# Expert outputs stored by row in DRAM and fetched by token, a mixture-of-experts gather in four parts, and dense up products with both activation parts in one matmul

## The chip, the core and the metric

The kernel runs on one core of a Trainium2 chip. The metric is the device time of one execution in microseconds (us). Five engines work side by side, each through its own instruction queue in order: TensorE (PE; its weight loads are listed apart as PEld), VectorE (DVE), ScalarE (ACT), GpSimd (POOL) and SyncE (SP, which here issues only transfers). An engine whose next instruction waits holds up everything behind it in its queue.

## What is computed

Two transformer-like blocks over 256 tokens of width 1024. The parts that the change touches:

```
def swiglu(h, w_gate, w_up, w_down):                      # dense, D_FF = 2816
    return (jax.nn.silu(h @ w_gate) * (h @ w_up)) @ w_down

def moe_swiglu(h, router_w, router_b, w_gate, w_up, w_down):   # 8 experts, top 2 per token
    ...
    out = jnp.zeros_like(h)
    for e in range(N_EXPERTS):
        out = out + gates[..., e:e + 1] * swiglu(h, w_gate[e], w_up[e], w_down[e])
    return out
...
# second block, MLP with D_FF_2 = 4096
m = jnp.einsum('bsf,fd->bsd', jnp.square(jax.nn.relu(jnp.einsum('bsd,df->bsf', h, w_up[l]))), w_down[l])
```

In order: a convolution block (A), the dense swiglu (B), attention (C), the mixture of experts (D), a mixer of attention and a gated delta net (F), and the MLP (G).

## The kernel before

**Two-part products.** Every float32 operand of a large product is split in a rounded high part and a low remainder (`split`: ACT copies the high part, DVE subtracts). A product is three matmuls, high by high, high by low, low by high (`mm3`), summed in PSUM. Weights come in tiles of 1 MiB (`raw`, a ring of 4 buffers, transfers issued by SP); each is split in two halves of 1024 columns (`whi` by ACT, `wlo` by DVE, rings of 6), so PE's matmuls wait for ACT and DVE, and SP's next transfer waits for DVE to be done with a `raw` buffer.

**Dense up products** (blocks B and G). The normalised activations lie transposed in SBUF, high parts in two tiles (`hhi`), low parts in two others (`hlo`). One up product of 256 features (`lin_feat`) runs over 2 feature halves and 8 slices of the model width, 3 matmuls of 256 columns each: 48 matmuls into one PSUM bank of 512 columns. Block B makes 22 of them (gate and up in 11 chunks), block G 15 in this way (the first of its 16 chunks goes through `lin_first`, which stays). After them DVE multiplies the bank by the norm's factor, ACT takes the silu, and so on, and the down product of the chunk before follows (24 matmuls of 512 columns).

**Mixture of experts** (`moe_block`). An expert has room for 128 tokens. For a pair of experts a one-hot matrix `G` (DVE) picks the tokens: `gather` multiplies it with the stored activations (32 matmuls of 256 columns, in 4 banks, each emptied by ACT and DVE into `xg`). Each expert then has 11 chunks: 24 matmuls of 512 columns into `pgu` (gate and up side by side), `gated` (ACT, then DVE) into `msg`, two transposes (`mpt`), a split into `mhi` and `mlo`, and the down product, 12 matmuls into the expert's two `acc` banks. The transposes and the down product of a chunk are emitted inside the next chunk. After an expert's last down product `scatter` splits `acc` (ACT `yhi`, DVE `ylo`), multiplies it with the transposed one-hot `GT` (8 matmuls of 512 columns, `scat`), and DVE adds gate times result to the residual `x` in 4 instructions. A branch in expert 0 (`overflow`) holds a second pass for experts with more than 128 tokens. In the last expert the constants of the mixer are loaded through POOL (`mixer_consts`).

**What sets the order.** The Tile framework orders each engine's instructions when the program is built; `tc.issue_after` pins single ones. In a chunk the two transposes stand either after 12 of the 24 `pgu` matmuls or right after the first; the built order of before has them after 12 in 57 of the 88 chunks and after the first in 31.

Of the kernel before, what the change touches and what calls it, by code (L numbers as in the profile page):

```python
# [14 lines left out]
P = 128  # L15
# [17 lines left out]
def _const_tables():  # L33
# [30 lines left out]
    put("low", np.tile((e[None, :] < e[:, None]).reshape(1, 64), (P, 1)))  # L64
    put("qsc", np.where(p < 8, 0.125, 1.0)[:, None])
# [37 lines left out]
def kernel(ctx: ExitStack, tc: tile.TileContext, ins: dict, out: bass.AP):  # L103
# [244 lines left out]
    class Feed:  # L348
# [3 lines left out]
        def __init__(self, *gains):  # L352
            self.gains, self.views, self.wait, self.rs, self.bc = gains, None, [], [None, None], {}
            self.early, self.pre = {}, {}
            self.stats, self.stats_late = [], False

        def piece(self, tb, half, x):
            if self.views is None:
                self.views = [hT_view(*hT_tiles("h")) for _ in self.gains]
# [26 lines left out]
        def convert(self, g, tb, half, ps_):  # L386
            hi, lo = self.views[g]
# [398 lines left out]


    def ffn_block(x, feed, nxt):
# [218 lines left out]
    def moe_block(x, feed, nxt):  # L1007
# [28 lines left out]
        def one_hots(e):  # L1036

            G = [wk("G", T, F32R) for _ in range(2)]
            for j in range(2):
                for tb in range(2):  # L1040
# [6 lines left out]
        def gather(G, n, hi, lo):  # L1047

            per = 512 // n
            for b in range(KD // per):  # L1050
# [10 lines left out]

        def scatter_mat(G, GT, r, ps_):

            for tb in range(2):
                pe.transpose(ps_[:, tb * P:(tb + 1) * P], f(G[tb]), ident)
            for tb in range(2):
                mm(ps_[:, 256:257], f(G[tb]), rs[tb], tb == 0, tb == 1)
            act.activation(GT, ps_[:, :T], AF.Copy)
            act.activation(r, ps_[:, 256:257], AF.Copy)

        def gated(sg, pgu, r):
            act.activation(sg, pgu[:, 0:256], AF.Silu, scale=r)  # L1072
            stt(sg, pgu[:, 256:512], r, sg, ALU.mult, ALU.mult)
# [85 lines left out]

        jobs = {}  # L1160

        def start(e):
            if e % 2 == 0:
                jobs["G"] = one_hots(e)
                hi, lo = [[b4("xg", F32R) for _ in range(2)] for _ in range(2)]
                jobs["pair"] = [[t[k // 4][:, (k % 4) * 256:(k % 4 + 1) * 256] for k in range(KD)] for t in (hi, lo)]
                gather(jobs["G"], 256, *jobs["pair"])
            o = slice((e % 2) * P, (e % 2 + 1) * P)
            J = dict(xg=[[t[:, o] for t in h] for h in jobs["pair"]], r=sm("rse", 1, bufs=3),
                     GT=kpool.tile([P, T], F32R, tag="gt", name=nm("GT"), bufs=2),  # L1170
# [11 lines left out]
        def down(p):  # L1182
# [9 lines left out]
            if c == NCH - 1:  # L1192
# [5 lines left out]
        pend = None  # L1198
        start(0)
        for e in range(NE):  # L1200
            for c in range(NCH):
# [10 lines left out]
                gated(sg, pgu, J["r"])  # L1212
# [484 lines left out]
    def mlp_block(x, feed, nxt):  # L1697
# [17 lines left out]
        for c in range(n):  # L1715
# [19 lines left out]
    def feed_of(st):  # L1735
# [20 lines left out]
        fd.soon = st == "G"  # L1756
# [101 lines left out]
```

## Time and profile before

| | us |
|---|---|
| median of 3 runs | 1704.89 |
| lowest, highest run | 1704.25, 1707.17 |
| the profiled execution, its own time | 1699.43 |
| span of the profiled execution | 1697.7 |
| PE busy in the span | 1625.0 (96%) |
| DVE busy | 1250.7 (74%) |
| ACT busy | 1016.9 (60%) |

The span runs from the first to the last instruction; the time of an execution has 1.7 us more around it. Busy shares are averages over stages with different limits. The mixture of experts fills the span from about 471 to 1282 us, block B about 140 to 340 us, block G about 1505 to 1690 us.

### The profile page before, as it was taken

What the parts mean: (1) busy time and instruction counts of PE and PEld (TensorE: products, weight loads), DVE (VectorE), ACT (ScalarE), POOL (GpSimd) and SP (SyncE); (2) the same over time, 40 slices, a digit from 0 to 9 for tenths busy, and PEclk for the clock granted to TensorE, in tenths of its full rate; (3) what the DMA queues carried; (4) which work ended last, traced back from release to release, by engine and by line L of the source; (5) the groups of instructions that cost most, each with busy time, mean ns of one, the idle gap of its engine ahead of it and who ended that gap; (6) DMA issues with size and microseconds to landing.
All of it is one profiled execution on the core that took longest, in us unless ns stands there. A gap on an engine that the chain in (4) does not pass through costs nothing.

```text
span 1697.7 us, 26302 instructions
## 1 busy us (share of the span) xinstructions
PE 1625.0 (96%) x10450; PEld 1375.9 (81%) x10450; DVE 1250.7 (74%) x1738; ACT 1016.9 (60%) x1464; POOL 78.9 (5%) x113
## 2 busy tenths in 40 slices
PE   7999999999889999999999999999998988989998
PEld 6769999898778788777878778787777877879997
DVE  4466555676578998989988898989887775385554
ACT  4245444565467777777777777777676454354442
POOL 2400000000000000000000000000000000011111
PEclk9989999999899999999999999999999998999999
DMA  6655555435528889999999998899995341035551
GB/s 237 186 181 192 178 194 177 175 133 199 199 103 324 323 335 355 343 351 352 335 337 352 373 356 335 338 349 341 361 354 186 125 142 46 3 139 200 196 180 45
DMA packets 59973, 408.71 MB, mean 241 GB/s; under 512 B 7353, under 2 KB 7745, under 8 KB 12609
## 3 DMA queue, kind: packets, MB, share of 16 engines
q1 hardware_dynamic: 56448, 396.86, 63.4%
q0 software_dynamic: 3104, 9.55, 2.0%
q8 instruction: 85, 1.39, 0.3%
q10 hardware_dynamic: 288, 0.52, 0.1%
q14 instruction: 48, 0.39, 0.1%
HBM read 404.67 MB, written 2.24 MB: 240 GB/s over the span
## 4 chain that ended last, share of the span: by engine, by line
PE 60%; DVE 5%; ACT 3%; issue 2%; DMA 1%; POOL 0%; DVEq 0%; POOLq 0%; ACTq 0%
PE pgu L145 27%; PE acc L145 18%; PE pu L145 6%; DVE wlo L156 2%; PE pi L145 2%; PE paq L145 1%; ACT whi L167 1%; PE pqkv L145 1%; PE mpt L1178 1%; PE scat L145 1%; DMA raw<-in_moe_w_down_dram 1%; ACT xg L1058 0%; DVE qkv L159 0%; DVE Vi L156 0%; PE po L145 0%
## 5 line engine op out<-in xcount | busy, mean ns | idle before, releaser
L156 DVE TENSOR_TENSOR wlo<-raw,whi 128x1024 fp32r<-128x1024 f32 x752 | 890.8, 1222 | 254.7 <-ACT whi L167 246.8
L167 ACT ACTIVATE whi<-raw 128x1024 fp32r<-128x1024 f32 x752 | 761.1, 1057 | 256.0 <-PE pu L145 71.8
L145 PE MATMUL pgu<-whi,xg 128*128 128x512 f32 x1408 | 467.7, 398 | 5.9 <-DVEq L1106 4.1
L145 PEld LDWEIGHTS pgu<-whi,xg 128*128 128x128 f32 x1408 | 265.6, 189 | 63.2 <-PEq L1106 4.4
L145 PE MATMUL pgu<-wlo,xg 128*128 128x512 f32 x704 | 283.8, 403 | 1.1 <-issue 1.0
L145 PEld LDWEIGHTS pgu<-wlo,xg 128*128 128x128 f32 x704 | 132.9, 189 | 39.6 <-DVE wlo L156 13.2
L145 PE MATMUL acc<-wlo,mhi 128*128 128x512 f32 x352 | 135.1, 391 | 1.1 <-DVE wlo L156 1.1
L145 PE MATMUL acc<-whi,mlo 128*128 128x512 f32 x352 | 134.4, 389 | 0.0
L145 PE MATMUL acc<-whi,mhi 128*128 128x512 f32 x352 | 127.1, 390 | 1.4 <-ACT whi L167 1.4
L145 PE MATMUL pu<-hlo,whi 128*128 128x256 f32 x432 | 122.3, 283 | 0.5 <-DVE hlo L159 0.5
L145 PE MATMUL pu<-hhi,whi 128*128 128x256 f32 x432 | 122.2, 283 | 0.0
L145 PE MATMUL pu<-hhi,wlo 128*128 128x256 f32 x432 | 122.2, 283 | 0.0
L1072 ACT ACTIVATE msg<-pgu,rse 128x256 f32<-128x256 f32 x88 | 41.8, 475 | 81.1 <-PE pgu L145 81.1
L145 PE MATMUL acc<-wlo,fhi 128*128 128x512 f32 x216 | 85.1, 394 | 0.0
L145 PE MATMUL acc<-whi,fhi 128*128 128x512 f32 x216 | 85.0, 394 | 0.0
L145 PE MATMUL acc<-whi,flo 128*128 128x512 f32 x216 | 85.0, 394 | 0.0
L167 ACT ACTIVATE mhi<-mpt 128x256 fp32r<-128x256 f32 x88 | 33.9, 385 | 84.5 <-PE mpt L1178 84.5
L145 PEld LDWEIGHTS pu<-hlo,whi 128*128 128x128 f32 x432 | 82.7, 191 | 1.3 <-DVE hlo L159 0.7
L145 PEld LDWEIGHTS pu<-hhi,whi 128*128 128x128 f32 x432 | 82.6, 191 | 0.6
L145 PEld LDWEIGHTS pu<-hhi,wlo 128*128 128x128 f32 x432 | 82.7, 191 | 0.0
L145 PEld LDWEIGHTS acc<-wlo,mhi 128*128 128x128 f32 x352 | 66.1, 188 | 17.1 <-DVE wlo L156 3.3
L145 PEld LDWEIGHTS acc<-whi,mhi 128*128 128x128 f32 x352 | 65.9, 188 | 15.8 <-ACT whi L167 2.0
(400 smaller groups left out, 2640.8 us busy)
## 6 DMA issues: line engine op xcount, KB each, us to landing
raw<-in_moe_w_gu_dram SPq DMA_DIRECT2D x172, 1024.0 KB, 6.4
raw<-in_moe_w_down_dram SPq DMA_DIRECT2D x86, 1024.0 KB, 6.3
raw<-in_w_up_dram SPq DMA_DIRECT2D x16, 1024.0 KB, 4.8
raw<-in_w_down_dram SPq DMA_DIRECT2D x16, 1024.0 KB, 4.9
raw<-in_w_in_dram SPq DMA_DIRECT2D x14, 1024.0 KB, 4.8
raw<-in_ffn_w_gate_dram SPq DMA_DIRECT2D x11, 1024.0 KB, 4.9
raw<-in_ffn_w_up_dram SPq DMA_DIRECT2D x11, 1024.0 KB, 4.8
raw<-in_ffn_w_down_dram SPq DMA_DIRECT2D x11, 1024.0 KB, 4.8
```

The costliest lines, as they stand in the source:

```text
L145: last_pe[0] = pe.matmul(o, l, r, start=start, stop=stop, skip_group_check=True).ins
L156: return (eng or dve).tensor_tensor(out=o, in0=a, in1=b, op=op)
L167: return act.activation(hi, src, AF.Copy), tt(lo, src, f(hi), ALU.subtract, eng)
L1072: act.activation(sg, pgu[:, 0:256], AF.Silu, scale=r)
L1178: pe.transpose(pt[:, j * P:(j + 1) * P], p["sg"][:, j * P:(j + 1) * P], ident)
```

## The change

Three edits. (1) In blocks B and G an up product runs per feature half into a bank of its own, with the activations' high and low parts side by side in one tile (`hT_pairs`), so that the high weights meet both in one matmul of 512 columns; the two halves of the bank are then added by `halves` (ACT copies one out, DVE adds the other). (2) For experts 0 to 6 the scatter is replaced by a store of the expert's 128 output rows to a DRAM tile `yrows` (`store`: two ACT copies and a transfer issued by ACT). `addresses` works out in expert 0, for each token, the row of its first and second expert and the two gates; `fetch` reads them back in expert 7 with four indirect transfers of POOL, 128 rows of 4 KB each, and `combine` adds gate times row to `x`, four DVE instructions of 1024 columns behind the `gated` instructions of chunks 4 and 5. Expert 7 keeps its scatter. A token's expert that is 7, or that has no room, points to a row of zeros. (3) The gather of a pair is made in four parts, in chunks 3 to 6 of the expert before it, instead of all at once after chunk 5, and `start` comes after chunk 7; `mixer_consts` moves from chunks 1, 4, 7 to 3, 6, 8.

```
+    def lin_bank(ps_, W, hT, nb):
+        c = slice(nb * P, (nb + 1) * P)
+        for k in range(KD):
+            mm(ps_, W[0][k][:, c], hT[2][k], k == 0, False)
+            mm(ps_[:, :T], W[1][k][:, c], hT[0][k], False, k == KD - 1)
...
+    def hT_pairs():
+        both = [v3(b4("h", F32R), 512)[:, j, :] for _ in range(4) for j in range(2)]
+        return [[t[:, :T] for t in both], [t[:, T:] for t in both], both]
...
+    def halves(o, ps_):
+        act.activation(o, ps_[:, T:], AF.Copy)
+        tt(o, o, ps_[:, :T], ALU.add)
...                                             (ffn_block)
-            pg, pu = bank("pg"), bank("pu")
-            lin_feat(pg, feed.take(("g", c), lambda: wcols(wg, c)), hT)
-            lin_feat(pu, feed.take(("u", c), lambda: wcols(wu, c)), hT)
             sg, su = wk("fsg", 512), wk("fsu", 512)
-            tt(v3(sg, T), v3(pg, T), feed.R2(), ALU.mult)
-            act.activation(sg, sg, AF.Silu)
-            tt(v3(su, T), v3(pu, T), feed.R2(), ALU.mult)
+            for key, w, o in (("g", wg, sg), ("u", wu, su)):
+                W = feed.take((key, c), lambda: wcols(w, c))
+                for nb in range(2):
+                    ps_ = bank("p" + key)
+                    lin_bank(ps_, W, hT, nb)
+                    halves(o[:, nb * T:(nb + 1) * T], ps_)
+                if key == "g":
+                    tt(v3(sg, T), v3(sg, T), feed.R2(), ALU.mult)
+                    act.activation(sg, sg, AF.Silu)
             tt(sg, sg, su, ALU.mult)
+            tt(v3(sg, T), v3(sg, T), feed.R2(), ALU.mult)
...                                             (moe_block)
+        def store(e, acc):
+            y = b4("y")
+            for nh in range(2):
+                act.activation(y[:, nh * 512:(nh + 1) * 512], acc[nh], AF.Copy)
+            nc.scalar.dma_start(yrows[e * P:(e + 1) * P, :], y)
...
+        def fetch():
+            back["rows"] = [b4("yr") for _ in range(4)]
+            for i, t in enumerate(back["rows"]):
+                pool.indirect_dma_start(t[:], None, yrows[:, :],
+                                        bass.IndirectOffsetOnAxis(ap=back["at"][:, i:i + 1], axis=0))
+
+        def combine(i):
+            varop[0] = stt(x[i // 2], back["rows"][i], back["g"][:, i:i + 1], x[i // 2], ALU.mult, ALU.add).ins
...
-            if c == NCH - 1:
+            if c == NCH - 1 and e < NE - 1:
+                store(e, J["acc"])
+            elif c == NCH - 1:
                 scatter(J["acc"], b4("yhi", F32R), b4("ylo", F32R), J["GT"],
...
-                if e == NE - 1 and c in (1, 4, 7):
-                    mixer_consts(c // 3)
-                if c == NCH // 2 and e + 1 < NE:
+                if (e, c) == (0, 1):
+                    addresses()
+                if e == NE - 1:
+                    if c == 1:
+                        fetch()
+                    if c in (4, 5):
+                        with tc.issue_after(gate_op):
+                            combine(2 * c - 8)
+                        with tc.issue_after(varop[0]):
+                            combine(2 * c - 7)
+                    if c in (3, 6, 8):
+                        mixer_consts((3, 6, 8).index(c))
+                if e % 2 and e + 1 < NE and 3 <= c < 7:
+                    if c == 3:
+                        pair_hots(e + 1)
+                    gather(jobs["G"], 256, *jobs["next"], part=c - 3)
+                if c == 7 and e + 1 < NE:
                     start(e + 1)
...                                             (mlp_block, all chunks but the first)
-                pu = bank("pu")
-                lin_feat(pu, Wu, hT)
-                stt(v3(rl, T), v3(pu, T), 0.0, feed.R2(), MX, ALU.mult)
+                for nb in range(2):
+                    pu = bank("pu")
+                    lin_bank(pu, Wu, hT, nb)
+                    halves(rl[:, nb * T:(nb + 1) * T], pu)
+                stt(v3(rl, T), v3(rl, T), 0.0, feed.R2(), MX, ALU.mult)
```

How the built order moves. First PE in block B, inside an up product (`pu`), before (`hhi`, `hlo` are the activations' parts, `whi`, `wlo` the weights'):

```order
L145 MATMUL pu_1459<-hhi_1267,whi_1520 128x256
L145 MATMUL pu_1459<-hlo_1269,whi_1520 128x256
L145 MATMUL pu_1459<-hhi_1267,wlo_1521 128x256
L145 MATMUL pu_1459<-hhi_1267,whi_1520 128x256
L145 MATMUL pu_1459<-hlo_1269,whi_1520 128x256
L145 MATMUL pu_1459<-hhi_1267,wlo_1521 128x256
```

The same place of the changed kernel, where `h` holds both parts:

```order
L147 MATMUL pu_1502<-h_1267,whi_1494 128x512
L147 MATMUL pu_1502<-h_1267,wlo_1495 128x256
L147 MATMUL pu_1502<-h_1268,whi_1494 128x512
L147 MATMUL pu_1502<-h_1268,wlo_1495 128x256
L147 MATMUL pu_1502<-h_1269,whi_1494 128x512
```

Each three matmuls of 256 columns have become one of 512 and one of 256; PE has 592 matmuls fewer in the two blocks.

Second, PE at the end of expert 4's last down product (the `acc` rows), inside the first chunk after expert 5's first, before:

```order
L145 MATMUL acc_8759<-wlo_10094,mhi_10058 128x512
L145 MATMUL acc_8759<-whi_10093,mlo_10059 128x512
L145 MATMUL scat_10115<-yhi_10109,GT_8757 128x512
L145 MATMUL scat_10119<-yhi_10109,GT_8757 128x512
L145 MATMUL scat_10123<-yhi_10109,GT_8757 128x512
L145 MATMUL scat_10127<-yhi_10109,GT_8757 128x512
L145 MATMUL scat_10115<-ylo_10110,GT_8757 128x512
L145 MATMUL scat_10123<-ylo_10110,GT_8757 128x512
L145 MATMUL scat_10119<-ylo_10110,GT_8757 128x512
L145 MATMUL scat_10127<-ylo_10110,GT_8757 128x512
L145 MATMUL pgu_10131<-whi_10134,xg_8700 128x512
```

The same kind of place of the changed kernel on PE (expert 2), and then on ACT, whose queue now holds the store:

```order
L147 MATMUL acc_6849<-wlo_8005,mhi_7969 128x512
L147 MATMUL acc_6849<-whi_8004,mlo_7970 128x512
L147 MATMUL pgu_8024<-whi_8027,xg_6483 128x512
L1245 MATMUL mpt_8047<-cm,msg_7995 128x128 x2
L147 MATMUL pgu_8024<-wlo_8028,xg_6483 128x512
```

```order
L169 ACTIVATE whi_8031<-raw_8025 128x1024
L1195 ACTIVATE y_8020<-acc_6848 128x512
L1195 ACTIVATE y_8020<-acc_6849 128x512
L169 ACTIVATE mhi_8050<-mpt_8047 128x256
L1196 DMA yrows<-y_8020 128x1024
L169 ACTIVATE whi_8056<-raw_8054 128x1024
```

PE goes from the last `acc` straight into the next `pgu`; on ACT the two copies stand ahead of `mhi`, and the transfer behind it, ahead of the next `whi`. The transposes stand right behind the first `pgu` here: in the changed order this is so in 57 chunks (31 before), one transpose stands there and one after 12 in 8, and both after 12 in 23.

Third, DVE in expert 7 behind the `gated` instruction of chunk 4 (`msg`), in the changed kernel:

```order
L161 SCALAR_TENSOR_TENSOR msg_11885<-pgu_11833,rse_11261,msg_11885 128x256
L161 SCALAR_TENSOR_TENSOR x_4200<-yr_11661,atg_4680,x_4200 128x1024
L158 TENSOR_TENSOR wlo_11916<-raw_11913,whi_11915 128x1024
L161 SCALAR_TENSOR_TENSOR x_4200<-yr_11662,atg_4680,x_4200 128x1024
L158 TENSOR_TENSOR wlo_11920<-raw_11913,whi_11919 128x1024
L158 TENSOR_TENSOR mlo_11939<-mpt_11935,mhi_11938 128x256
```

Two `combine` instructions have come between the `wlo` of one chunk; the other two stand so in chunk 5. On POOL the four fetches stand ahead of the mixer's constants, which in the trace of before go out in experts 4 and 5 already.

## Rows read from the trace of the kernel before

**Rows 1.** Stages (windows): busy us (and count) of each engine, clock, DMA share, GB/s.
```profile
580.00:781.00 201.00, 199.72 (x897) 159.42 (x898) 182.86 (x201) 150.24 (x193) 0.00 (x0) 1.00 0.92 344
1515.00:1679.00 164.00, 164.00 (x1058) 149.28 (x1057) 93.44 (x92) 70.47 (x76) 28.61 (x15) 1.00 0.50 176
```

**Rows 2.** Chain that ended last, in block G: start us, us, piece.
```profile
1526.35 5.74 PE pu L145 x48
1532.09 5.47 PE acc L145 x24
```

**Rows 3.** The same chain in expert 1: a chunk with its transposes after 12.
```profile
636.48 2.73 PE pgu L145 x12
...
642.20 2.72 PE acc L145 x12
644.91 2.72 PE pgu L145 x12
```

**Rows 4.** The same chain in expert 2: transposes after the first matmul.
```profile
725.65 0.23 PE pgu L145
...
734.29 0.23 PE pgu L145
```

**Rows 5.** Timeline of DVE and PEld in that chunk: start us, us, idle before.
```profile
727.50 4.63 DVE L156 TENSOR_TENSOR wlo<-raw,whi 128x1024 fp32r<-128x1024 f32 x4 [0.38 <-ACT whi L167]
728.78 0.19 PEld L145 LDWEIGHTS pgu<-wlo,xg 128*128 128x128 f32 x1 [0.34 <-DVE wlo L156]
```

**Rows 6.** Timeline at expert 2's scatter: PE, ACT, DVE, PE.
```profile
777.25 0.39 PE L145 MATMUL acc<-whi,mlo 128*128 128x512 f32 x1
777.22 1.08 ACT L167 ACTIVATE yhi<-acc 128x512 fp32r<-128x512 f32 x2
779.97 2.73 DVE L159 SCALAR_TENSOR_TENSOR x<-scat,gates,x 128x512 f32<-128x512 f32 x4
780.77 0.50 PE L145 MATMUL pgu<-whi,xg 128*128 128x512 f32 x1
```

**Rows 7.** The chain: first `pgu` after the scatters of experts 0 and 6, and the last scatter.
```profile
580.01 3.02 PE pgu L145 x12
...
1182.51 3.02 PE pgu L145 x12
...
1279.31 2.39 PE scat L145 x8
```

**Rows 8.** Groups of 580 to 1180 us: busy us, mean ns, idle before and its releasers.
```profile
L156 DVE TENSOR_TENSOR wlo<-raw,whi 128x1024 fp32r<-128x1024 f32 x396 | 462.6, 1219 | 41.2 <-ACT whi L167 38.9
L167 ACT ACTIVATE whi<-raw 128x1024 fp32r<-128x1024 f32 x395 | 392.7, 1055 | 13.1 <-DMA raw<-in_moe_w_down_dram 10.8 <-DMA raw<-in_moe_w_gu_dram 1.1 <-DVE x L159 0.6
L167 ACT ACTIVATE mhi<-mpt 128x256 fp32r<-128x256 f32 x66 | 25.5, 387 | 68.4 <-PE mpt L1178 68.4
L156 DVE TENSOR_TENSOR mlo<-mpt,mhi 128x256 fp32r<-128x256 f32 x66 | 27.6, 418 | 4.7 <-ACT mhi L167 4.1
```

**Rows 9.** Timeline of POOL in block G's last chunks.
```profile
1657.96 1.89 POOL L156 TENSOR_TENSOR fsg<-fsg 128x512 f32<-128x512 f32 x1 [9.42 <-DVE fsg L159]
```

**Rows 10.** Issues of POOL and ACT: KB each and us to landing; duration of one (ns).
```profile
reltmp<-relscr POOLq DMA_DIRECT2D x2, 512.0 KB, 10.5
...
L517 ACTq DMA_DIRECT2D out_dram<-x x2: 338/358/378, 1689.8 to 1692.6; - x2
```

**Rows 11.** The chain at a gather, and the gather's DVE group (lines): count, busy us, mean ns.
```profile
622.81 0.97 PE xg L145 x8
...
L159 DVE SCALAR_TENSOR_TENSOR xg<-xg,cm,xg 128x256 fp32r<-128x256 f32 x24 | 9.9, 476 | 1.5 <-ACT xg L1058 1.5
```

**Rows 12.** Windows between pauses, and the fullest ones: columns as in Rows 1.
```profile
717.00:775.00 58.00, 58.00 (x258) 45.91 (x257) 51.83 (x54) 44.03 (x56) 0.00 (x0) 1.00 0.95 357
960.00:980.00 20.00, 19.77 (x86) 15.15 (x85) 18.16 (x19) 15.88 (x21) 0.00 (x0) 1.00 1.00 378
1230.00:1235.00 5.00, 4.47 (x19) 3.10 (x18) 3.36 (x5) 3.62 (x5) 0.00 (x0) 1.00 1.02 428
```

More of the change, by code (lines that the diff above doesn't have):

```diff
@@ L358, in piece @@
             if self.views is None:
-                self.views = [hT_view(*hT_tiles("h")) for _ in self.gains]
+                self.views = [hT_pairs() if self.paired else hT_view(*hT_tiles("h")) for _ in self.gains]
             ps_ = bank("tr", "acc")
@@ L1038, in one_hots @@
             G = [wk("G", T, F32R) for _ in range(2)]
-            for j in range(2):
-                for tb in range(2):
+            for tb in range(2):
+                for j in range(2):
                     k = tb * NE + e + j
@@ L1045, in moe_block, with gather @@
         ffn_gain = gain_of("ffn_norm", KD)
-        def gather(G, n, hi, lo):
+        def gather(G, n, hi, lo, part=None):
             per = 512 // n
-            for b in range(KD // per):
+            for b in range(KD // per) if part is None else (part,):
                 ps_ = bank("xg")
@@ L1064, in scatter_mat @@
             for tb in range(2):
+                mm(ps_[:, 256:257], f(G[tb]), rs[tb], tb == 0, tb == 1)
+            act.activation(r, ps_[:, 256:257], AF.Copy)
+            if GT is None:
+                return
+            for tb in range(2):
                 pe.transpose(ps_[:, tb * P:(tb + 1) * P], f(G[tb]), ident)
-            for tb in range(2):
-                mm(ps_[:, 256:257], f(G[tb]), rs[tb], tb == 0, tb == 1)
             act.activation(GT, ps_[:, :T], AF.Copy)
-            act.activation(r, ps_[:, 256:257], AF.Copy)
         def gated(sg, pgu, r):
             act.activation(sg, pgu[:, 0:256], AF.Silu, scale=r)
-            stt(sg, pgu[:, 256:512], r, sg, ALU.mult, ALU.mult)
+            return stt(sg, pgu[:, 256:512], r, sg, ALU.mult, ALU.mult).ins
         def scatter(acc, yhi, ylo, GT, gate, bk, after=None):
@@ new lines, in moe_block, with addresses @@
+        back = {}
+        def addresses():
+            row, at, g = sm("row", 16, bufs=1), sm("at", 4, bufs=1), sm("atg", 4, bufs=1)
+            ok, junk = sm("rowok", 16, bufs=1), sm("rowj", 16, bufs=1)
+            each = lambda n: C(n)[:, None, :].to_broadcast([P, 2, NE])
+            stt(v3(ok, NE), v3(posx, NE), P + 0.5, each("early"), ALU.is_lt, ALU.mult)
+            tt(v3(row, NE), v3(posx, NE), each("row0"), ALU.add)
+            tt(row, row, ok, ALU.mult)
+            for i in range(4):
+                c = slice(i // 2 * NE, (i // 2 + 1) * NE)
+                stt(junk[:, c], rk[:, c], float(i % 2), row[:, c], ALU.is_equal, ALU.mult, accum_out=at[:, i:i + 1])
+                stt(junk[:, c], rk[:, c], float(i % 2), gates[:, c], ALU.is_equal, ALU.mult, accum_out=g[:, i:i + 1])
+            ts(at, at, float(ZERO), None, ALU.add)
+            back["at"], back["g"] = spool.tile([P, 4], I32, tag="ati", name="ati", bufs=1), g
+            dve.tensor_copy(back["at"], at)
@@ L1160, in moe_block, with pair_hots @@
+        def fetch():
[5 more added lines that the diff above has]
+            varop[0] = stt(x[i // 2], back["rows"][i], back["g"][:, i:i + 1], x[i // 2], ALU.mult, ALU.add).ins
         jobs = {}
+        def pair_hots(e):
+            jobs["G"] = one_hots(e)
+            hi, lo = [[b4("xg", F32R) for _ in range(2)] for _ in range(2)]
+            jobs["next"] = [[t[k // 4][:, (k % 4) * 256:(k % 4 + 1) * 256] for k in range(KD)] for t in (hi, lo)]
@@ L1162, in start @@
         def start(e):
+            o = slice((e % 2) * P, (e % 2 + 1) * P)
             if e % 2 == 0:
[L1164 to L1168, printed above, removed]
+                jobs["pair"] = jobs["next"]
             J = dict(xg=[[t[:, o] for t in h] for h in jobs["pair"]], r=sm("rse", 1, bufs=3),
-                     GT=kpool.tile([P, T], F32R, tag="gt", name=nm("GT"), bufs=2),
+                     GT=kpool.tile([P, T], F32R, tag="gt", name=nm("GT"), bufs=1) if e == NE - 1 else None,
@@ L1198, in moe_block @@
         pend = None
+        pair_hots(0)
+        gather(jobs["G"], 256, *jobs["next"])
         start(0)
@@ L1211, in moe_block @@
                 sg = wk("msg", 256)
-                gated(sg, pgu, J["r"])
+                gate_op = gated(sg, pgu, J["r"])
                 if pend:
```

13 lines of the change are left out of this document (10 added, 3 removed).

## Prediction

> **What bounds the kernel now.** I read the stages first, by windows [rows 1]: in block G (and block B alike) PE is busy all of 164 us, with DVE at 93 and the transfers at half load, so PE alone bounds the dense blocks. In the two experts of 580 to 781 us PE is busy 199.72 of 201 us, but DVE 182.86 too and the transfers 0.92 of the time. There a PE saving counts only as far as DVE, ACT and the transfers keep up.
>
> Then the chain, for the price of one matmul. In block G 48 matmuls of 256 columns take 5.74 us, 119.6 ns each [rows 2]; in expert 1 twelve of 512 columns take 2.72 us, 226.7 ns each [rows 3]. So a matmul costs about 0.42 ns a column and 13 ns besides.
>
> Third, the chunk of an expert. With the transposes after 12 matmuls it repeats after 644.91 - 636.48 = 8.43 us [rows 3]; with the transposes after the first, after 734.29 - 725.65 = 8.64 us [rows 4]. In that chunk DVE waited 0.38 us for ACT before four `wlo`, and PE's weight load then waited for the first of them [rows 5]: ACT takes the weights up only behind `mhi`, `mhi` waits for the transposes, and PE needs that weight 12 matmuls later. The 0.21 us are a loop through three queues, not work on PE.
>
> Fourth, the end of an expert [rows 6]: the last `acc` matmul ends at 777.25 + 0.39 = 777.64 us, the next `pgu` starts at 780.77. The scatter holds PE for 3.1 us, of which 8 x 0.227 = 1.8 are matmuls. Six experts, 1 to 6, take 1182.51 - 580.01 = 602.5 us, a pair 200.8; expert 7 to its scatter takes 1279.31 - 1182.51 = 96.8 [rows 7].
>
> **The change, part by part.**
>
> Dense up products. Eight slices by two halves make 16 triples a product, 22 + 15 = 37 products. A triple costs 3 x 119.6 = 358.8 ns, its successor 226.7 + 119.6 = 346.3 [rows 2, 3]; 12.5 ns x 592 = **-7.4 us**. Nothing shows a 512-column matmul alternating with a 256-column one, so the bounds are 0 (the shorter one waits for its weights) and -7.4; I take -7.4, since the 256-column stream already changes weights each 119.6 ns. The added ACT copies and DVE adds (about 0.39 and 0.42 us each, the price of 256 columns out of PSUM [rows 8]) lie under PE's 100%: DVE has 70 us to spare in block G [rows 1], and 30 adds of 0.42 us come there. The exit of the last chunk becomes some 0.8 us longer; a POOL square of 1.89 us [rows 9] and three steps of 512 columns stand there (twice the 256-column price, 0.8 each), and 24 `acc` matmuls of 5.47 us [rows 2] cover the sum of about 5.1. Uncovered it would cost 0.8.
>
> A rule of the Trainium skill speaks against this term. TensorE: Matmul & The Clock Gate, section "Wait — 56ns, not 53.3ns?", puts the fixed part of a warm matmul at about 2.5 ns; by that the term would be an estimated 592 x 2.5 ns = 1.5 us. The rows give 13 ns, and the sum goes by them.
>
> End of experts 0 to 6. Removed: scatter, 3.1 us each. Added: on ACT two copies, 1.08 us by the two `yhi` of the same shape [rows 6], and a transfer's issue, 0.36 us by ACT's one now [rows 10]. The copies can start when `acc` ends, 0.23 + 0.22 us (one `pgu`, two transposes) before `mhi` could; so `mhi` and the weights queued behind it on ACT come 1.08 + 0.36 - 0.45 = 1.0 us later, and as PE waits for those weights within the chunk [rows 5], it waits 1.0. Bounds 0 and 1.4; I take 1.0.
>
> Gather. Its 32 matmuls stay, 4 x 0.97 us on PE [rows 11]; DVE's part, 8 x 0.476 us and some 0.9 of one-hots, now falls into chunks that DVE nearly fills. I take 4.6 a pair (bounds 3.9 and 4.7).
>
> A pair is then 20 chunks of 8.64 (the built order has the transposes early in most), 2 of 8.43, 4.6 of gather and 2 x 1.0 of stores: 172.8 + 16.9 + 4.6 + 2.0 = 196.3 against 200.8. Three pairs: **-13.6 us**. Expert 0 gains 3.1 - 1.0 at its end, and pays four early chunks (0.8) and `addresses`, a dozen tiny DVE instructions, mostly in DVE's wait for the first gather (bounds 0 and 3, taken 0.3): **-1.0**.
>
> Expert 7 pays. Five more early chunks: 1.1. Four `combine` of 1024 columns, 1.22 us each by `wlo` [rows 8], 4.9 in all in two chunks where DVE has about 0.6 us of waits each (41.2 us in 66 chunks [rows 8]): 3.7. The fetch brings 2.1 MB, and since it stands first on POOL, about 1 MB of mixer constants now follow it here, out of experts 4 and 5. How long an indirect transfer takes no row shows: nearest are POOL's 512 KB with short pieces, 10.5 us to land [rows 10]. Issued about 18 us into the expert (behind the last store), even two waves of 10.5 land by 39, while the first `combine` stands at 4.7 chunks, 41 us. So I take no wait for landing, but 2.5 us for the crowding of 3 MB. **+7.3 us** (bounds 1 and 21, the latter if the four came one after another: 18 + 42 = 60, 19 after the place).
>
> Sum: -7.4 - 13.6 - 1.0 + 7.3 = -14.7 us. Against the profiled execution's 1699.4 that is 1684.7; the median of the runs shown is 5.5 us above that execution, so **1690** by it.
>
> **The rivals.**
>
> *The chunk goes at 8.43 throughout.* Then the 0.21 us of early chunks fall: 60 in experts 1 to 6, 12.6 us, and with 2 us in experts 0 and 7 the time is 1675.5. For it: PE has no more to do in either order. Against: every early chunk between 717 and 775 us takes the longer time; 258 listed matmuls fill all 58 us [rows 12].
>
> *The dense products save nothing*, the lower bound above, because in the new stream the shorter matmul waits for its weights as long as the third matmul took: 1690 + 7.4 = 1697.5. For it: only this mixture of widths is unseen. Against: weight loads keep up with a new one each 119.6 ns now [rows 2]. The fixed part that the Trainium skill's page TensorE: Matmul & The Clock Gate gives (section named above) would lead close to this rival, to an estimated 1696.
>
> *Transfers become the bound, and the kernel slower.* Scatters and whole gathers are pauses in which weights catch up. Three pairs need 3 x (66 MiB of weights + 1 MiB stored) = 210.8 MB, expert 7 33 MiB, the fetch and some 2 MB of constants, 38.8 MB: 249.6 in all. At the 344 GB/s that a pair has now [rows 1] this takes 725 us against 699.3 [rows 7], and with the other terms (-7.4 and -1.0) the kernel ends at 1722. It decides below 249.6 / (699.3 + 8.4) = 353 GB/s. For it: 13.1 us in which ACT already waits for transfers [rows 8]. Against: 357 GB/s over 58 us without a pause, 378 over 20 and 428 over 5 [rows 12]. The Trainium skill, SBUF — State Buffer, section "A bandwidth-pool intuition that's wrong", gives a core about 358 GB/s of HBM and calls it nearly always the bottleneck: an estimated 697 us, thus 1694. The 378 and 428 lie above that figure.
>
> *The fetch is late.* Then the first `combine` holds DVE, all `wlo` behind it, and so PE; at the bound of 21 the time is 1704, no change. It decides when the rows land later than 41 us into expert 7.
>
> **How the numbers follow.** Chances: the forecast 0.48, chunks at 8.43 0.20, dense products saving nothing 0.14, transfers 0.10, late fetch 0.08. The likeliest gives 1690, own range 1682 to 1697. Eight in ten reach from the fast rival with its slack, 1673, to 1703, just short of the late fetch's bound. About 0.2%, 3.4 us, is what a measurement here can tell from no change. Faster by more: the first three and some of the late fetch, 0.84; the same 0.07 (late fetch and weak transfers); slower 0.09.
>
> **What would show it.** Right, if in the profile after: an up product's 32 matmuls take 5.54 us; from the last `acc` to the next `pgu` PE does not pause; pairs take about 196 us and the transfers' rate between stores is about 357 GB/s; in expert 7, chunks 4 and 5 are some 1.9 us longer. Wrong, if ACT's waits for `raw` grow well past 13 us, if DVE waits for `yr` before `combine`, if chunks with early transposes take 8.43, or if ACT's store holds `whi` by several us.

## The result, and the profile after

The median fell from 1705.36 us (1704.25 to 1707.17, 4 runs) to **1683.62 us** (1682.06 to 1684.81, 4 runs): ratio 0.9876, 95% interval [0.9861, 0.9892], that is 18 to 24 us less. The profiled execution took 1683.93 us with a span of 1681.8; against the one of before (1699.43, span 1697.7) that is 15.5 less.

The stages of the changed kernel by windows (columns as in [rows 1]): block G, experts 1 and 2, the stretch that answers to the first of [rows 12], the 30 us behind the fetch, expert 0's first chunks, the mixer as a whole and a late piece of it.

```profile
1501.00:1665.00 164.00, 164.00 (x831) 138.59 (x830) 112.99 (x124) 82.46 (x106) 17.32 (x16) 1.00 0.51 177
572.00:767.00 195.00, 194.33 (x880) 156.42 (x879) 175.75 (x190) 151.00 (x192) 0.00 (x0) 1.00 0.96 360
709.00:767.00 58.00, 58.00 (x259) 46.29 (x258) 52.28 (x55) 44.64 (x56) 0.00 (x0) 1.00 0.98 365
1165.00:1195.00 30.00, 27.00 (x114) 20.01 (x113) 22.83 (x24) 18.45 (x24) 7.67 (x8) 1.00 1.01 388
498.00:513.00 15.00, 10.54 (x41) 8.54 (x41) 8.13 (x9) 7.26 (x9) 0.00 (x0) 0.89 0.66 230
1262.00:1494.00 232.00, 205.92 (x2328) 182.12 (x2328) 146.20 (x326) 107.68 (x219) 7.13 (x13) 0.94 0.27 94
1474.00:1493.00 19.00, 15.18 (x56) 12.00 (x56) 10.86 (x24) 7.51 (x19) 1.12 (x2) 0.82 0.18 67
```

Two experts now need 195 us instead of 201, at 360 GB/s instead of 344, and PE still has almost no pause there; PE alone bounds block G as before. The chain that ended last in block G answers to [rows 2]:

```profile
1512.74 5.55 PE pu L147 x32
1518.29 5.48 PE acc L147 x24
1523.77 5.64 PE pu L147 x32
```

The up product's piece is 0.10 to 0.19 us shorter than the 5.74 of before, `acc` is what it was. From here the instructions by tile: the stores' copies and transfers, expert 7's scatter, the fetch (durations in ns, first and last start in us):

```profile
L1195 ACT ACTIVATE y<-acc x14: 592/595/597, 572.1 to 1156.0; 128x512 f32<-128x512 f32 x14
L147 PE MATMUL scat<-yhi,GT x4: 392/449/502, 1261.8 to 1263.3; 128*128 128x512 f32 x4
DMA to landing us min/median/max: 9.8/12.7/15.9
```

The first and the last copy tell how long six experts take: 1156.0 - 572.1 = 583.9 us, against 602.5 [rows 7]; from the last copy to the scatter expert 7 takes 105.8, against 96.8. (PE's own chunks give 583.4 and 106.0.) The third line is the fetch's: issued at 1165 to 1170 us, all rows have landed by 1186.

The timeline (start us, us, idle before and what ended it) at three places, with lines left out between: block B's first product; the end of expert 1 and the chunks behind it; and in expert 7 the fetch, ACT's waits, two `combine` with POOL's wait for one of the constants between them, and PE's wait for the mixer's table.

```profile
133.81 0.50 PE L147 MATMUL pg<-h,whi 128*128 128x512 f32 x1 [0.82 <-DVE h L161]
...
671.16 0.39 PE L147 MATMUL acc<-whi,mlo 128*128 128x512 f32 x1
671.39 0.39 PE L147 MATMUL pgu<-whi,xg 128*128 128x512 f32 x1
671.62 0.38 PE L1245 MATMUL mpt<-cm,msg 128*128 128x128 f32 x2
672.11 0.39 ACT L169 ACTIVATE mhi<-mpt 128x256 fp32r<-128x256 f32 x1
...
689.06 0.38 PE L1245 MATMUL mpt<-cm,msg 128*128 128x128 f32 x2
...
697.74 0.38 PE L1245 MATMUL mpt<-cm,msg 128*128 128x128 f32 x2
...
706.38 0.38 PE L1245 MATMUL mpt<-cm,msg 128*128 128x128 f32 x2
...
1165.01 1.40 POOL L1219 DMA_INDIRECT yr<-yrows,ati  x1 [708.91 <-DVE msg L161]
...
1177.40 2.01 ACT L169 ACTIVATE whi<-raw 128x1024 fp32r<-128x1024 f32 x2 [1.22 <-DMA raw<-in_moe_w_down_dram]
1181.16 2.01 ACT L169 ACTIVATE whi<-raw 128x1024 fp32r<-128x1024 f32 x2 [1.32 <-DMA raw<-in_moe_w_gu_dram]
1184.93 2.01 ACT L169 ACTIVATE whi<-raw 128x1024 fp32r<-128x1024 f32 x2 [1.49 <-DMA raw<-in_moe_w_gu_dram]
1188.88 2.01 ACT L169 ACTIVATE whi<-raw 128x1024 fp32r<-128x1024 f32 x2 [1.95 <-DMA raw<-in_moe_w_down_dram]
1192.64 1.27 DVE L161 SCALAR_TENSOR_TENSOR x<-yr,atg,x 128x1024 f32<-128x1024 f32 x1
1196.12 1.06 POOL L598 CAST hsel<-hsel 48x1024 fp32r<-48x1024 f32 x1 [22.53 <-DMA hsel<-in_c_sel_dram]
1196.21 2.06 DVE L161 SCALAR_TENSOR_TENSOR x<-yr,atg,x 128x1024 f32<-128x1024 f32 x1
1229.87 1.10 PE L147 MATMUL rel<-reltmp,cm 128*128 128x512 f32 x2 [1.52 <-DMA reltmp<-relscr]
```

Where [rows 6] had 3.1 us without a `pgu` matmul, `pgu` follows `acc` after 0.23 us. A chunk repeats after 706.38 - 697.74 = 8.64 us, as in [rows 4]; the two chunks that follow a store take 689.06 - 671.62 = 17.44, 0.16 more than 2 x 8.64. The groups of 572 to 1156 us answer to [rows 8]:

```profile
L158 DVE TENSOR_TENSOR wlo<-raw,whi 128x1024 fp32r<-128x1024 f32 x398 | 465.4, 1220 | 50.5 <-ACT whi L169 48.7
L169 ACT ACTIVATE whi<-raw 128x1024 fp32r<-128x1024 f32 x397 | 393.8, 1052 | 11.8 <-DMA raw<-in_moe_w_gu_dram 5.2 <-DMA raw<-in_moe_w_down_dram 3.7 <-DVE wlo L158 2.8
```

ACT waits for the weights' transfers no longer than before (8.9 us, 11.9 before), and DVE has about 10 us more of waits for ACT (48.7, 38.9 before): the pairs got shorter and their feeding engines did not fill up.

Expert 7 is where the change pays. While the fetch and the constants land, a 1 MiB piece of weights becomes ready only every 3.8 us (1177.40, 1181.16, 1184.93, 1188.88), though the transfers move 388 GB/s; a chunk of 8.64 us needs three. The first `combine` starts 6 us after the last row has landed.

The sums of stages, each between PE's first matmuls of it in the two timelines (us):

| stretch | before | after | difference | forecast |
|---|---|---|---|---|
| start to block B's first product | 131.9 | 133.8 | +1.9 | 0 |
| block B's products | 191.6 | 187.7 | -3.9 | -4.4 |
| attention and routing | 145.5 | 145.1 | -0.4 | 0 |
| expert 0, to expert 1's second chunk | 111.0 | 105.8 | -5.2 | -1.0 |
| to expert 7's second chunk (three pairs) | 602.5 | 583.4 | -19.1 | -13.6 |
| expert 7 to its scatter | 96.8 | 106.0 | +9.2 | +7.3 |
| mixer, to block G's first product | 228.5 | 232.6 | +4.1 | 0 |
| block G | 189.8 | 187.4 | -2.4 | -3.0 |

### The profile page after: what moved, and what is told of

It is laid out like the page before. It is cut to its first block, busy times and chain, and to the rows that moved or that the text cites. A ratio compares the mean times of both kernels' runs of the same rounds, so it can differ in the third digit from the quotient of the medians.

```text
span 1681.8 us, 25138 instructions
## 1 busy us (share of the span) xinstructions
PE 1605.4 (95%) x9788; PEld 1335.3 (79%) x9788; DVE 1268.6 (75%) x1795; ACT 1042.2 (62%) x1531; POOL 74.3 (4%) x119
## 5 line engine op out<-in xcount | busy, mean ns | idle before, releaser
L147 PE MATMUL pgu<-whi,xg 128*128 128x512 f32 x1408 | 459.5, 395 | 5.7 <-PEq L1131 4.5
L147 PE MATMUL pgu<-wlo,xg 128*128 128x512 f32 x704 | 288.4, 410 | 5.6 <-DVE wlo L158 5.5
L147 PE MATMUL pu<-h,whi 128*128 128x512 f32 (+1 forms) x448 | 153.2, 388 | 0.5 <-DVE h L161 0.5
L147 PE MATMUL pu<-h,wlo 128*128 128x256 f32 x432 | 121.0, 280 | 0.0
L147 PEld LDWEIGHTS pu<-h,whi 128*128 128x128 f32 x448 | 83.1, 188 | 19.1 <-DVE h L161 0.7
L147 PEld LDWEIGHTS pu<-h,wlo 128*128 128x128 f32 x432 | 81.6, 189 | 0.6
L147 PEld LDWEIGHTS acc<-whi,mlo 128*128 128x128 f32 x352 | 66.1, 188 | 13.1
L147 PE MATMUL pg<-h,whi 128*128 128x512 f32 x176 | 62.3, 396 | 0.8 <-DVE h L161 0.8
```

What stands on the lines that cost most here:

```text
L147: last_pe[0] = pe.matmul(o, l, r, start=start, stop=stop, skip_group_check=True).ins
```

## The experiments

Times between stores and scatter are read as above, from the first and last copy `y` and the first `scat`. The changed kernel's are 583.9 and 105.8.

**The dense products alone**, in the kernel before: the hunks on `lin_bank`, `hT_pairs`, `halves`, `ffn_block` and the MLP, none of `moe_block`.

> The kernel before with the dense up products alone in the new form. The forecast's theory: 592 triples at 12.5 ns less each give 7.4 us, ratio 0.9957. What the changed kernel's trace says since: a product of block G takes 5.71 to 5.81 us where it took 5.90, G's first product is built in the old form, and block B's first product starts 1.1 us later after its transposes; 22 + 14 products at 0.18 us less the 1.1 give 5.4 us, ratio 0.9968. The rival that the shorter matmul waits for its weights: no change. The fixed part that the Trainium skill's page TensorE: Matmul & The Clock Gate, section "Wait — 56ns, not 53.3ns?", gives would leave an estimated 1.5 us.

Measured: ratio 0.9954 [0.9939, 0.9970], 5.1 to 10.4 us less. The chain in its block G shows the same pieces:

```profile
1515.81 5.65 PE pu L145 x32
...
1527.03 5.55 PE pu L145 x32
```

The rival without a gain is out, and so is the estimated 1.5 us from the Trainium skill's page TensorE: Matmul & The Clock Gate (section "Wait — 56ns, not 53.3ns?", some 2.5 ns of fixed part a matmul): here an up product, from its first matmul to the next stage's, takes 5.61 us on average where it took 5.75 (in block G and block B alike, by PE's timeline, here and in the changed kernel). That is 0.143 / 16 = 8.9 ns a triple, some 70% of the 12.5 forecast from the row. PE's count fell from 10450 matmuls to 9858, 592 fewer, so all 22 + 15 products are in the new form: block G's chunk through `lin_first` is not one of the 15, and the 14 of the expectation is one too few. The run also gives expert 0 its proper base: in this kernel, whose experts are those of before, expert 0's stretch takes 108.9, not 111.0.

**The gather in one piece**, the stores kept:

```
-                if e % 2 and e + 1 < NE and 3 <= c < 7:
-                    if c == 3:
-                        pair_hots(e + 1)
-                    gather(jobs["G"], 256, *jobs["next"], part=c - 3)
+                if e % 2 and e + 1 < NE and c == NCH // 2:
+                    pair_hots(e + 1)
+                    gather(jobs["G"], 256, *jobs["next"])
```

> The changed kernel with each later gather in one piece in the middle of experts 1, 3 and 5, as before; the stores and the dense products stay. Theory: in one piece the gather stops PE until DVE has caught up with its part, as in the kernel before (the chunk with the gather lasts 13.8 there, 5.4 more than its neighbours), while the four parts cost 3.2 us together in the changed kernel (37.8 us for the four chunks against 4 x 8.64); so a pair gets 2.2 us longer, 6.5 us in all, ratio to the kernel before about 0.991. Rival: the gather costs PE its 32 matmuls wherever it stands, and nearly all of the gain of the experts is the scatter's; then the ratio stays within 0.001 of the changed kernel's 0.988. Second rival: a pause lets the weights catch up, and the whole gather is as fast or faster.

Measured: ratio 0.9902 [0.9883, 0.9922]; its interval overlaps that of the changed kernel. Six experts take 585.5, 1.6 more and not 6.5. In the timeline of PE the whole gather stands without a pause:

```profile
811.45 0.28 PE L147 MATMUL xg<-G,xh 128*128 128x256 f32 x1
...
815.28 0.40 PE L147 MATMUL pgu<-whi,xg 128*128 128x512 f32 x1
```

32 matmuls in 3.83 us. The first rival holds for nearly all: the four parts are worth some 0.5 us a pair, the gain of the experts is the scatter's.

**Late transposes throughout**:

```
+            with tc.issue_after(last_pe[0]):
                 for j in range(2):
                     pe.transpose(pt[:, j * P:(j + 1) * P], p["sg"][:, j * P:(j + 1) * P], ident)
```

> The changed kernel with the two transposes of each chunk held behind its first twelve pgu matmuls throughout; 57 of 88 chunks had them behind the first matmul. The loop theory of the forecast (the 0.21 us of a chunk with early transposes are a loop through ACT and DVE): chunks take 8.43 throughout, 57 x 0.21 = 12 us less, about 1672 us, ratio 0.981. Rival: the transfers bound the pairs at what they reach now; 3 MiB in 8.64 us are 364 GB/s, 8.43 us want 373, and then ACT waits for raw grow and the pairs stay at 194. Between: chunks at 8.43 save what the transfers allow; at 366 GB/s nothing, at 373 all.

Measured: ratio 0.9897 [0.9877, 0.9917], no gain; six experts 587.0, 3.1 more. PE's and PEld's timeline after expert 1's store:

```profile
674.69 0.38 PE L1246 MATMUL mpt<-cm,msg 128*128 128x128 f32 x2
684.27 0.38 PE L1246 MATMUL mpt<-cm,msg 128*128 128x128 f32 x2
690.20 0.19 PEld L147 LDWEIGHTS pgu<-wlo,xg 128*128 128x128 f32 x1 [0.25 <-DVE wlo L158]
692.84 0.38 PE L1246 MATMUL mpt<-cm,msg 128*128 128x128 f32 x2
```

A chunk takes 8.57 here, not 8.43: another `wlo` is late then, and the weight load waits 0.25 us for DVE (in 65 us of expert 6 it does so 8 times, 2.3 us in all). ACT waits 0.3 us for transfers in the same 65 us, so neither named theory is right: not the transfers bound them, and the loop through ACT and DVE is not left behind by a later transpose. The chunk with the store takes 9.58: with `mhi` late, the store costs the 1.0 us of the forecast, which the early order hides.

**Five stores left out** (`store` returns at once for experts 1 to 5; zeros are written to their rows early).

> The changed kernel without the two copies and the transfer that store the results of experts 1 to 5; their rows are zeros, written once, early, so the output lacks these experts. Experts 0 and 6 store as in the changed kernel. Price of a store: the forecast gave 1.0 us; in the changed kernel's trace the chunk after the store (the expert's second) takes 9.01 us and others with early transposes 8.64, 0.37 more. Theory: the store is that 0.37, and the second chunk of experts 2 to 6 falls to 8.64 while that of experts 1 and 7 stays at 9.01. Rival: the 9.01 is not the store's (the weights of that chunk are late by themselves), and it stays everywhere. Second rival: ACT's 1.4 us slow the transfers' requests for several chunks, and the whole expert gets shorter by 1.0 or more.

Measured, PE's timeline after expert 1's end:

```profile
671.68 0.38 PE L1252 MATMUL mpt<-cm,msg 128*128 128x128 f32 x2
...
688.96 0.38 PE L1252 MATMUL mpt<-cm,msg 128*128 128x128 f32 x2
```

The first theory was right on its chunk (8.64 after the missing stores, 9.01 where they stayed), but the next chunk, which the store had pushed into the late order at 8.43, now takes 8.64 too: 17.28 for both, 0.16 less. Six experts take 583.6; a store costs 0.1 to 0.2 us.

**What expert 7 pays.** Four edits and their expectations, then one table.

```
consts_early, consts_early_spread:
-                    if c in (3, 6, 8):
-                        mixer_consts((3, 6, 8).index(c))
+                if (e, c) in ((6, 3), (6, 6), (7, 8)):
+                    mixer_consts(((6, 3), (6, 6), (7, 8)).index((e, c)))
no_combine:
-                    if c in (4, 5):
-                        ...
combine_spread, consts_early_spread:
+                    if 5 <= c < 9:
+                        with tc.issue_after(gate_op):
+                            combine(c - 5)
```

> The changed kernel with the mixer's constants loaded in expert 6 (chunks 3 and 6) ahead of the fetch on POOL, and their last matmuls in chunk 8 of expert 7 as now. Measured so far: from expert 7's second chunk to its scatter 106.0 us in the changed kernel, 96.8 before, the forecast said 104.1. Theory of the transfers: between 1165 and 1195 us the fetch's 2.1 MB and 1 MB of constants stand beside the weights at a DMA share of 1.0, and ACT waits 1.2 to 2.0 us for raw four times; 1 MB at 0.38 MB a us less gives 2.7 us, and the 1.5 us that PE waits for reltmp are gone too: about 102 us there, and expert 6 grows by less than 1. Theory of DVE: the four combine hold DVE and nothing changes but the 1.5: 104.5. Rival: expert 6 has no room either and pays what expert 7 saves.

> The changed kernel with the fetch but without the four combine that add the fetched rows to x, so the output lacks the experts 0 to 6. Theory of DVE: four combine of 1.27 us are in the way of the weights' wlo, and the stretch from expert 7's second chunk to its scatter falls from 106.0 us by nearly their 5.1, to 101. Theory of the transfers: the weights are late by themselves in those chunks and DVE waits for them anyhow; then it falls by less than 2.

> The changed kernel with one combine in each of chunks 5 to 8 of expert 7 instead of two in chunks 4 and 5. Theory of DVE (a chunk has about 0.6 us of slack for it, so 2.5 us cost 1.9 and 1.27 cost 0.7): the stretch from expert 7's second chunk to its scatter falls by 1.0 to 3.0, to 103 to 105. Theory of the transfers: the two chunks with late weights hide part of a combine and chunks 7 and 8 do not; it stays at 106 or grows to 107.

> Both edits, the constants in expert 6 and one combine in each of chunks 5 to 8. Where transfers and DVE each cost their part, the savings add: 106.0 less 4 for the constants and 1 to 3 for the combine, 99 to 101 from expert 7's second chunk to its scatter, and the ratio to the kernel before falls by 0.003 to 0.985. Rival: one covers the other, and it equals the better of the two alone.

| kernel | ratio | six experts | expert 7 to scatter | chunks 1 to 7 | chunk 8 | behind it |
|---|---|---|---|---|---|---|
| changed | 0.9876 [0.9861, 0.9892] | 583.9 | 105.8 | 69.2 | 13.5 | 23.4 |
| constants early | 0.9878 [0.9858, 0.9897] | 588.6 | 102.6 | 66.8 | 11.7 | 24.3 |
| no `combine` | - | 584.1 | 103.5 | 68.0 | 11.5 | 24.2 |
| `combine` spread | 0.9874 [0.9856, 0.9892] | 584.7 | 104.1 | 69.6 | 11.4 | 23.3 |
| both | 0.9859 [0.9844, 0.9874] | 588.9 | 99.8 | 65.3 | 11.4 | 23.3 |

The last three columns are read from the first `pgu` matmul of each chunk; chunks are counted from 0. Two things have to be taken out of the sums before an edit is credited.

The first is the clock. In the last 15 us ahead of the scatter the granted clock was 0.91 without `combine`, as the window below shows, and 0.91 with the constants early, against 1.00 in the changed kernel; the stretch behind chunk 8 is 0.8 to 0.9 us longer for it. In chunks 1 to 7 it was 1.00 in all but `combine` spread, 0.98.

```profile
1245.50:1260.85 15.35, 13.41 (x53) 9.79 (x51) 11.83 (x14) 9.28 (x12) 0.00 (x0) 0.91 0.90 319
```

The second is chunk 8, which holds the matmuls of the mixer's table. A row of the table is worked out ahead (PE `rel`, then DVE `relrow`), and POOL sends it out (`relscr`) and brings the table back (`reltmp`). The timeline of it in the changed kernel, and then without `combine`:

```profile
1206.82 0.81 PE L147 MATMUL rel<-ohn,rb 32*8 32x384 f32 x2
1214.20 0.54 DVE L158 TENSOR_TENSOR relrow<-rel,ohn 8x384 f32<-8x384 f32 x1
1215.04 0.54 POOL L604 DMA_DIRECT2D relscr<-relrow  x1 [17.80 <-DVE relrow L158]
...
1207.70 0.81 PE L147 MATMUL rel<-ohn,rb 32*8 32x384 f32 x2
1208.70 0.54 DVE L158 TENSOR_TENSOR relrow<-rel,ohn 8x384 f32<-8x384 f32 x1
```

`relrow` starts 7.4 us after PE's matmul in the changed kernel, behind the second `combine` of the chunk, `mlo` and five `wlo`, and 1.0 us after it without `combine`; POOL stood idle until then. So the 2.0 us by which chunk 8 is shorter are `combine`'s too, by way of DVE's queue. How much of it is their busy time and how much the later place of `relrow` in the built order no run tells apart, and other runs with `combine` in chunks 4 and 5 have chunk 8 at 11.6 to 13.6 at full clock. With the clock's 0.8 left out the four `combine` cost 1.2 us in chunks 1 to 7 and up to 2.0 in chunk 8, up to 3.2 in all, between the two theories (less than 2, nearly 5.1). The rest is hidden, since weights are late in those chunks anyhow. One of ACT's waits in the run without them:

```profile
1196.01 2.00 ACT L169 ACTIVATE whi<-raw 128x1024 fp32r<-128x1024 f32 x2 [3.06 <-DMA raw<-in_moe_w_gu_dram]
```

With the constants early, chunks 1 to 7 are 2.4 us shorter and chunk 8 1.7: with the clock's 0.9 left out expert 7 takes the 102 of the theory of the transfers. But the constants did not land in expert 6, where the code has them: POOL issued them between 779 and 857 us, in experts 3 and 4; only the table's transfers (1109 to 1117 us) fell into expert 6:

```profile
778.86 0.56 POOL L196 DMA_DIRECT2D gfin<-in_rows_dram  x1 [322.09 <-DMA raw<-in_moe_w_down_dram]
853.87 0.53 POOL L588 DMA_DIRECT2D ohn<-in_c_oh_dram  x1 [74.45 <-PE pgu L147]
```

The six experts grow by 4.7 us: 1.8 in experts 3 and 4, 1.6 in expert 6 (0.7 of it a matmul of the table that moved along), 0.5 in expert 7's first chunk, and 0.6 in a chunk of expert 2 ahead of all of it. So the rival holds in its kind: others pay what expert 7 saves. Spreading `combine` alone shows in chunk 8 only; with the constants away it gives 1.5 us in chunks 1 to 7 (66.8 to 65.3), and both edits together reach 100, within the 99 to 101 where each part costs its own.

**Extra reads** in experts 2 and 4, `dve.memset` on a spare tile behind chunk 3's gate product and `pool.dma_start` of 512 KB into it, two and four times.

> The changed kernel with additional reads that nobody uses, into spare buffers, issued on POOL behind chunk 3's gate product: two of 512 KB in expert 2 and four in expert 4, 1.05 and 2.1 MB. Experts 2, 4 and 6 last 95.5 to 95.8 us in the changed kernel, and the runs with the constants in expert 6 were 1.8 and 2.1 us longer in the pairs where 1 MB of them landed. Theory that the transfers are all but full between the stores (a chunk's 3 MiB in 8.64 us are 364 GB/s): expert 2 grows by 1.05 / 0.364 = 2.9 us and expert 4 by 5.8, less some tenths that the buffers of raw cover. Rival: the transfers have room (419 GB/s were seen while the fetch ran), 2.1 MB cost at most 2.1 / 0.364 x (1 - 364/419) = 0.8, and what expert 7 pays is of another kind, the indirect form or the order on POOL.

Measured: expert 2 takes 97.5 (95.5 without), expert 4 98.9 (95.5): 2.0 and 3.4 us, 0.4 of the latter in a chunk ahead of the reads. Windows from the issue of the reads on (697.8 and 894.5 us), and the same chunks of expert 4 in the changed kernel:

```profile
698.00:716.00 18.00, 16.51 (x72) 12.77 (x71) 14.75 (x15) 12.44 (x16) 0.95 (x2) 1.00 0.99 389
895.00:914.00 19.00, 17.60 (x76) 13.28 (x75) 14.98 (x16) 11.98 (x16) 1.58 (x3) 1.00 1.01 410
...
891.00:910.00 19.00, 19.00 (x87) 15.09 (x86) 17.32 (x18) 14.14 (x19) 0.00 (x0) 1.00 0.96 354
```

Nearer to the full price (2.9 and 5.8) than to the rival's 0.8: the transfers rise from some 355 GB/s to 389 and 410, and the rest is paid. A chunk in a pair is therefore bound by PE with its small loop, but with too little room in the transfers for another 1 MB. This is one execution, and a single chunk is now and then 1 us late without an edit near it (expert 1's third in this run, 9.7 for 8.4). The fetch by itself is priced much like these plain reads: in the run with both edits above, where 2.1 MB of fetch land without the constants and ahead of any `combine`, chunks 3 and 4 take 10.8 and 10.4 us, 3.9 more than 2 x 8.64.

**Three more on the fetch**: a single indirect transfer instead of four; four plain ones from fixed rows; and the four indirect ones issued apart, behind a `memset` in chunks 1 to 4, with `combine` in chunks 5 to 8.

> The changed kernel with one indirect transfer of 512 KB instead of four; the four combine add that one tile, so the output has wrong rows for three of four. The stretch from expert 7's second chunk to its scatter was 106.0 us, 103.7 without the combine, 96.8 before the change. Theory of the bytes: 1.57 MB fewer at 0.38 MB a us give 4.1 us, 102. Theory of an order or a wait in expert 7 that hangs on the first landing: it stays at 106.

> The changed kernel with the four indirect transfers replaced by four plain ones of 512 KB from fixed rows, on the same queue at the same place, so the output adds wrong rows. Theory of the bytes: the stretch stays at 106.0 within 0.7. Theory of the form (one piece for each of 512 rows, addresses made by POOL): it falls by 2 or more.

> The changed kernel with the four indirect transfers issued one by one behind the gate products of chunks 1 to 4 of expert 7, and one combine in each of chunks 5 to 8. The stretch was 106.0 us in the changed kernel and 104.3 with the combine spread alone. Theory of the bytes: the burst after 1165 us is gone, but the same bytes pass, 38.8 MB in the expert; if weights are late only in the burst it falls to 101 to 103, if the whole expert is full of bytes it stays at 104. A version that is better than the changed kernel by 3 us would have a ratio of 0.986.

| kernel | ratio | six experts | expert 7 to scatter | chunks 1 to 7 | chunk 8 | behind it |
|---|---|---|---|---|---|---|
| one transfer | - | 583.8 | 104.6 | 68.1 | 13.5 | 23.4 |
| plain transfers | - | 586.9 | 106.3 | 67.8 | 15.4 | 23.4 |
| issued apart | 0.9868 [0.9851, 0.9884] | 584.2 | 104.1 | 68.1 | 11.7 | 24.5 |

Three quarters of the fetch less save 1.2 us, not 4.1. While only 0.5 MB and the constants land, weights are as late as with the whole fetch, by ACT's timeline in that run:

```profile
1178.46 2.00 ACT L169 ACTIVATE whi<-raw 128x1024 fp32r<-128x1024 f32 x2 [2.74 <-DMA raw<-in_moe_w_down_dram]
```

So bytes alone are not the measure there. What holds the weights back while the constants land, their few partitions (32 and 48) or the queue that they share with the fetch, no run told apart; it stays open. The plain transfers do not test the form as meant: their rows stand in fixed places, POOL issued three of the four as soon as experts 3 to 5 were stored (at 874.6, 971.4 and 1071.2 us, and the six experts are 3.0 us longer), and only one fell into expert 7. But this one can be set beside the run with one indirect transfer: each has 0.5 MB ahead of the same constants, and chunks 1 to 7 take 67.8 and 68.1 us, so the indirect form costs at most some tenths there. (Its 15.4 in chunk 8 were at a granted clock of 0.89.) Issued apart, the lateness moves from chunk 4 (10.0 instead of 12.8) to chunk 5 (13.5 instead of 11.2). Of its 104.1 the clock, 0.89 in the last 15 us, has 1.1, and in chunks 1 to 7 it was 0.97; that leaves 103 at most, the upper end of the last theory's first branch, and with clocks so different it does not decide between the two. No version here is measurably better than the changed kernel; all intervals overlap its own.

## Why the forecast was right, and where it was not

The range held the time and the sign was right. By its own execution the sum was -14.7 and the trace gave -15.5, but that nearness is luck: terms had compensated, and the clock had its part. Leaving out what the clock did (below), the change is worth -5.2 (dense: -3.9 - 2.4, and +1.1 of the table's first line), -3.1 (expert 0), -19.1 (pairs) and +9.2 (expert 7), together -18.2; the runs give -18 to -24.

- *Dense, -7.4 forecast, about -5.2 in the trace.* The mechanism was right, its size was not: a triple saves 8.9 ns instead of 12.5, and 592 of them 5.3 us; in the runs of the dense part alone the term is 5 to 10. Block B's first matmul needs both activation parts and waits 0.82 us for DVE's last `h`; that costs little, since before, PE paused behind its first two matmuls for the low part:

```profile
132.92 0.39 PE L145 MATMUL pg<-hlo,whi 128*128 128x256 f32 x1 [0.58 <-DVE hlo L159]
```

- *Pairs, 196.3 forecast, 194.5 measured.* Early chunks at 8.64 and the vanished pause came as foretold. Two terms were too dear: the store (1.0 a piece forecast, 0.1 to 0.2 by the run without stores; the copies delay `mhi`, but only the late order, 9.58 against 8.57, makes PE pay for it) and the gather (4.6 forecast; the four chunks with parts take 37.8, 3.2 more than 4 x 8.64).
- *Expert 0, -1.0 forecast, -3.1 against the base of the dense run.* The scatter's 3.1 went, and the store, the early chunks and `addresses` cost nothing that shows.
- *Expert 7, +7.3 forecast, +9.2 measured.* Near in sum, wrong in its parts. `combine` (3.7 forecast, in chunks 4 and 5) costs 1.2 in chunks 1 to 7, where late weights hide most of it, and up to 2.0 by the table's row behind it in DVE's queue, a path that the forecast did not have. The crowding was put too low: without `combine`, and without the clock's 0.8, expert 7 still takes 6.0 us more than before, where the forecast had 3.6 for early chunks and crowding together.
- *The step from the sum to the median.* The 5.5 us by which the profiled execution of before lay below its median were taken for a constant. They are the draw of one execution: before's later runs spread from 1698.9 to 1709.4. Without that step the forecast was 1684.7. (A smaller slip: the 13.1 us put down to ACT's waits for transfers are all of its idle time before `whi`; 11.9 are the transfers'.)

Of the rivals, chunks at 8.43 throughout were tried by late transposes and give 8.57; dense products without a gain are excluded; the fetch lands 6 us before its first use. The transfers as a bound came out as a near miss: they decide below 353 GB/s, the pairs run at 360, and with 1 MB more they pay 2 us. The Trainium skill's SBUF — State Buffer, section "A bandwidth-pool intuition that's wrong", gives about 358 GB/s of HBM a core and calls it almost always the bottleneck. The windows above show 388 GB/s over 30 us and 410 over 19, more than that figure. That the transfers are the place to look fits expert 7; that HBM is what holds the weights back there no run shows.

## What to carry to other kernels

Removing a pause on PE is worth its length only as far as the streams that used the pause have room; price the bytes that the replacement brings, and the stage in which they land, before its instructions. A delay on a feeding engine can cost next to nothing while the consumer's order leaves it slack (the store: 0.1 to 0.2 us of 1.0), so price it with the order that is built, and look for what else stands behind it in its queue (`relrow`). Take an experiment's stage length apart by chunk before crediting an edit: here 2 us of a wait for a table and up to 1.1 us of clock lay in the same stretch.

## What the hardware showed unexpectedly

**The granted clock moves whole stages.** The mixer (block F) is the same work in both kernels. The windows of before: the mixer as a whole, a late piece of it, and expert 0's first chunks.

```profile
1279.00:1508.00 229.00, 202.50 (x2334) 179.43 (x2334) 147.00 (x328) 108.79 (x222) 7.14 (x13) 0.96 0.27 95
1490.00:1507.00 17.00, 12.78 (x60) 10.42 (x61) 11.52 (x24) 7.52 (x19) 1.13 (x2) 1.00 0.21 77
500.00:515.00 15.00, 9.98 (x32) 7.21 (x31) 6.47 (x7) 5.98 (x8) 0.00 (x0) 0.77 0.56 196
```

The changed kernel's windows (first fence of the result) have 0.94 for the whole, PE 3.4 us longer busy, and 0.82 for the late piece, 1474 to 1493. PE had paused for the same 1.79 us ahead of the late piece in both; once it went on at the full 2.4 GHz, once partly at 1.2, and PE was busy 2.4 us longer in the piece. In expert 0, behind the pause of 4 us that both kernels have there, it was the other way: 0.77 before and 0.89 after, worth 2 us that are not the change's. The later runs confirm that it is a draw: all but the dense run keep the changed kernel's mixer, and it takes 227.8 to 233.6 us in them, 228.5 and 232.6 in the two executions above. Such draws, 2 to 4 us an execution, are as large as the terms that were to be told apart, and they reach into the stages that are compared chunk by chunk too: the last 15 us of expert 7 went at 1.00 in most runs and at 0.89 to 0.91 in three.

**POOL and DVE.** One of the four `combine` took 2.06 us instead of 1.27. It is the one during which POOL's `CAST` ran (1196.12 and 1196.21 us in expert 7's timeline). It was seen once and not tried apart.
